# Attention gated per pair of heads and stored beside the chunk gate's part, so that each out-projection tile loads one contiguous block

## The chip, the cores and the metric

One NeuronCore of a Trainium2 chip runs the whole program. The metric is the device time of one launch in microseconds (us). Three runs of the kernel before gave 1382.57, 1385.22 and 1387.93 us; the median is 1385.22 us. Everything else about it is read from one profiled execution, whose own device time was 1381.67 us and whose trace spans 1379.9 us from the first to the last instruction.

## What is computed

One inference step of a decoder layer with two parallel groups: forgetting attention (8 heads of 64) and a chunk gate (4 channel groups of 128). Both are gated by a silu, joined to 1024 features and projected out. Cut to what matters here:

```python
def merge(x, attn, za, mix, u, zc, w_out):
    a = attn.reshape(B, S, D_ATT) * silu(za)               # 512 attention features
    m = (u * mix).reshape(B, S, D_CHK) * silu(zc)          # 512 chunk-gate features
    return x + concatenate([a, m], axis=-1) @ w_out        # 1024 x 1024
```

The prompt has 2048 positions; eight sample positions of a decode step (paged cache of 512 rows each) run through the same layer beside it. Everything is float32. The products keep float32 accuracy by splitting each operand into a rounded high part and the rest, and adding three matmuls (high by high, high by low, low by high).

## The kernel before

**Stages.** The input projection comes first (to about 580 us of the trace). It writes the attention queries, keys and values, and the chunk gate's result, to DRAM scratch. The loop over `UNITS` follows (about 600 to 1180 us): a unit is one head `h` and one chunk `c` of 512 queries, `values` (L933). The order of units is head after head, at the end (6,2), (7,0), (6,3), (7,1), (7,2), (7,3). Between a unit's matmuls the generator `fill` slips in filler work that writes the PSUM bank `fl`: what is left of the gate projections, then the out weights, then the first out-projection tiles. The last phase (1191.78 us to the end) has the remaining out-projection tiles, 14 of 16, in the banks `sc` and `av`, two of each, and the sample's own tile.

**Who sets the order.** TensorE's (PE's) instructions are in the order in which the Python code emits them. The other engines are ordered by a list scheduler, and each then works strictly in that order: an instruction that waits holds up all behind it. `later(ns, fn)` (L144) delays a piece of work until PE's counted clock has moved on by `ns`, and `pump` (L150) runs what has come due. `pump(all_=True)` runs everything that is waiting at once. After the last unit, L1249 does that, and tile 8 of the out-projection does it again (L1112).

**The attention part.** A unit leaves its unnormalised result in scratch `aT` (L981, features by positions). Its row sums are added up in `acc` by GpSimd (POOL, L965), turned by `add_up` (L983: four transposes of `acc` into a `tp` bank, a VectorE (DVE) reduction and a reciprocal `sm`, L988 and L989). 2000 ns later `done` (L991) turns the reciprocals, ScalarE (ACT) copies them out (`rt`, L995), and SyncE (SP), whose queue issues nearly all transfers, stores 2 KB into scratch `rT` (L996). The three `tp` banks are shared with the running maxima of the scores (matmuls `tp<-k,q`, DVE reductions `mn`, L892).

**The out-projection.** A tile is 128 positions. `out_inputs` (L1045) issues six loads on SP's queue: `m4` from `mT` (chunk gate), `z4` from `zT` (the silu gate), `a4` from `aT`, twice `r4` from `rT` (each head's reciprocals broadcast to its 64 features) and `xy` (the residual `x`). The first five fetch a 128-column slice of a features-by-positions array, which is 512 contiguous bytes per row. `OLAG` (11000 ns) of PE's clock later, `parts` runs: POOL multiplies `z4` by `r4` (L1061), DVE multiplies `a4` by 0.5 and by that (L1065), ACT casts `m4` and `a4` to the high parts and DVE subtracts for the low parts (two casts and two subtractions of 128x512; helper `split`, L230 and L235), all into the tile `am`. `out_products` (L1071) then runs 24 matmuls for each half of 512 output features, and DVE adds the bank to `xy` (L1081), which frees the bank. `OAHEAD` = 3 tiles are asked for ahead. `load_out_weights` (L1023) loads and splits the out weights `wo`, `WOLAG` (7000 ns) after their loads.

**The chunk gate's part.** `zc_steps` (L489) ends with a store of 128 features by 512 positions to `mT`.

Of the kernel before, what the change touches and what calls it, by code (L numbers as in the profile page):

```python
# [19 lines left out]
P = 128  # L20
# [4 lines left out]
NH = 8  # L25
# [11 lines left out]
FILL = 0.50  # L37
FILL7 = 0.95
FLAG = 7000.0
WOLAG = 7000.0  # L40
WOSTEP = 1500.0
OLAG = 11000.0
SLAG = 3000.0
LAG = 6400.0
AVB = 8
# [12 lines left out]
OAHEAD = 3  # L58
KORDER = (4, 5, 6, 7, 0, 1, 2, 3)
WOENG = ('act',)  # L60
OFIRST = 1
PAIRS = (14,)
KSTART = 8
PACE = 800.0
# [11 lines left out]
def hymba_step(ctx, tc, x_prompt, x_sample, cache_k, cache_v, cache_logf, page_table, g_norm, w_in,  # L76
# [129 lines left out]
    qk_lo = dr.tile([2 * 512, SEQ], F32, name="qk_lo")  # L206
    v_st = dr.tile([NH, P, NT, HD], F32, name="v_st")
    mixT = dr.tile([512, SEQ], F32, name="mixT")
    mT = dr.tile([512, SEQ], F32, name="mT")
    zT = dr.tile([512, SEQ], F32, name="zT")  # L210
    aT = dr.tile([512, SEQ], F32, name="aT")
    kx = dr.tile([NH, 4, SEQ], F32, name="kx")
# [267 lines left out]
    def cols_of(t, f, cp):  # L480
        return t[f * P:(f + 1) * P, cp * 512:(cp + 1) * 512]

    def u_steps(unit, f0, f, cp, tag, mx):
        nc.sync.dma_start(mx, cols_of(mixT, f, cp))
        po = bank(tag)
        yield from feat_steps(po, unit, f0, cp)
        nc.vector.scalar_tensor_tensor(mx, mx, 0.5, po, op0=ALU.mult, op1=ALU.mult)

    def zc_steps(unit, f0, f, cp, tag, mx):  # L489
        po = bank(tag)  # L490
        yield from feat_steps(po, unit, f0, cp)
        sz = twice_silu(po)
        nc.gpsimd.tensor_tensor(mx, mx, sz, op=ALU.mult)
        nc.sync.dma_start(cols_of(mT, f, cp), mx)

    def za_steps(unit, f0, f, cp, tag):
        po = bank(tag)
# [131 lines left out]
    def decode_scores():  # L629
# [12 lines left out]
                yield DEC[0]  # L642
        nc.sync.dma_start(kept, keep)

    def decode_attention():
        keep = s8(t="keep")
        nc.sync.dma_start(keep[:, :512], kept)
        lfp, sc = gates_and_scores(keep)
        prT = keep[:, 512:896].rearrange("p (n m) -> p n m", n=NPG)
        nc.vector.memset(prT[:, :, BH:], 0.0)  # L650
        own = small(8)[:BH]
        nc.sync.dma_start(own[:, 0:1], tiny[0].rearrange("b (h o) -> (b h) o", o=1))
        nc.sync.dma_start(own[:, 1:2], tiny[1].rearrange("b (h o) -> (b h) o", o=1))
        yield 8000

        one, lfT, cc = (s2(t=t)[:BH] for t in ("one", "lfT", "cc"))
        nc.vector.memset(one, 1.0)
# [24 lines left out]
        pt = bank("tp")  # L682
        for g in range(NPG):
            transpose(pt[:, g * BH:(g + 1) * BH], lg[:, g * P:(g + 1) * P], ident[:BH, :BH])
        nc.scalar.copy(prT[:, :, :BH], pt[:, :NPG * BH].rearrange("p (n m) -> p n m", n=NPG))
        for b in range(B):
            hs = slice(b * NH, (b + 1) * NH)
            vb = s8(t="vb").rearrange("p (g f) -> p g f", g=NPG)
            page_loads(b, range(NPG), [(cv, lambda g: vb[:, g])])

            def summed(b=b, vb=vb):

                po = bank("tp")
# [3 lines left out]
                nc.scalar.copy(t, po)  # L697
                for g in range(NPG):
# [234 lines left out]
    def values(at):  # L933
# [3 lines left out]
        for kt in range(4 * c + 4):  # L937
# [31 lines left out]
            def step(kt=kt, p=p, n0=n0, acc=acc, c=c, st=st, at=at):  # L969

                if kt == 0:
                    st["av"] = bank("av")
                av, fin = st["av"], kt == 4 * c + 3
                e = kt % 2
                mm(av[e * HD:(e + 1) * HD, n0:], hd["vst"][:, kt], p[:, n0:], kt < 2, kt >= 4 * c + 2,
                   (512 - n0) * 0.844)
                if fin:
                    t = s2(t="at")
                    nc.scalar.copy(t[:HD], av[HD:])
                    nc.vector.tensor_tensor(t[:HD], t[:HD], av[:HD], op=ALU.add)  # L980
                    nc.sync.dma_start(aT[h * HD:(h + 1) * HD, c * 512:(c + 1) * 512], t[:HD])  # L981

                    def add_up():  # L983
                        pt = bank("tp")
                        for j in range(4):
                            transpose(pt[:, j * P:(j + 1) * P], acc[:, j * P:(j + 1) * P], ident)
                        rs = small(4)
                        nc.vector.tensor_reduce(rs, pt.rearrange("p (j k) -> p j k", j=4), axis=AX.X, op=ALU.add)  # L988
                        nc.vector.reciprocal(rs, rs)  # L989

                        def done():  # L991
                            pt = bank("tp")
                            transpose(pt[:4, :P], rs, ident)
                            t = s2(t="rt")[:4, :P]
                            nc.scalar.copy(t, pt[:4, :P])  # L995
                            nc.sync.dma_start(rT[h, c * 512:(c + 1) * 512].rearrange("(n p) -> n p", p=P), t)  # L996
                            if h == NH - 1:
                                finished[0] += 1
                                for i in range(OFIRST if finished[0] == 1 else 0):
                                    prepare(i)  # L1000
                        later(2000, done)
                    due[at % 2] = add_up
                    later(ACLAG, lambda: flush(at % 2, add_up))
# [35 lines left out]
        for n, k in enumerate(KORDER):  # L1039
            later(n * WOSTEP, lambda n=n, k=k: load(n, k))  # L1040

    def rows_of(t, t0):
        return t[:, t0:t0 + P].rearrange("(k p) t -> p k t", p=P)

    def out_inputs(i):  # L1045

        t0 = i * P
        az, xy = s4(t="az"), s4(t="xy")
        a4, z4 = (az[:, b * 512:(b + 1) * 512].rearrange("p (k t) -> p k t", k=4) for b in range(2))
        m4, r4 = (s2(t=t).rearrange("p (k t) -> p k t", k=4) for t in ("m4", "r4"))  # L1050
        nc.sync.dma_start(m4, rows_of(mT, t0))
        nc.sync.dma_start(z4, rows_of(zT, t0))
        nc.sync.dma_start(a4, rows_of(aT, t0))
        rv = rT[:, t0:t0 + P].rearrange("(k o) t -> o k t", o=2)
        for o in range(2):
            nc.sync.dma_start(r4[o * HD:(o + 1) * HD], rv[o].partition_broadcast(HD))
        nc.sync.dma_start(xy, x[t0:t0 + P])
        got = {}

        def parts():  # L1060
            nc.gpsimd.tensor_tensor(z4, z4, r4, op=ALU.mult)  # L1061
            am = s8(F32R, "am")
            hi, lo = (am[:, r * D:(r + 1) * D].rearrange("p (k t) -> p k t", k=KT) for r in range(2))
            split(hi[:, 4:], lo[:, 4:], m4, "act")
            nc.vector.scalar_tensor_tensor(a4, a4, 0.5, z4, op0=ALU.mult, op1=ALU.mult)  # L1065
            split(hi[:, :4], lo[:, :4], a4, "act")
            got.update(hi=hi, lo=lo, xy=xy)
        later(OLAG, parts)
        return got
# [27 lines left out]
    def out_tiles():  # L1097

        gs = None
        for i in range(NT):  # L1100
# [8 lines left out]
            if i == 8:  # L1109
                for _ in Pe.steps:  # L1110
                    pass
                pump(all_=True)  # L1112
                gs = decode_out()
            if gs is not None and i < 12:
                next(gs, None)
# [130 lines left out]
                fill(m * dose)  # L1246
                pump()
    run_av(0)
    pump(all_=True)  # L1249
    hold[0] = 0.0  # L1250
    last_phase[0] = True
    for _ in fgen:
# [31 lines left out]
```

## Time and profile before

| | us |
|---|---|
| median of three runs | 1385.22 |
| the profiled execution: device time | 1381.67 |
| the profiled execution: span of the trace | 1379.9 |
| PE busy in the span (95%) | 1311.9 |
| DVE busy (51%) | 704.4 |
| POOL busy (41%) | 572.0 |
| ACT busy (31%) | 434.3 |
| share of time of the DMA engines on SP's queue | 44.2% |

The page gives the busy time of each engine and the mean clock that PE was granted (0.981 of full speed over the span). PE is busy nearly all the time, so what matters is where it is not, and where its clock is low. A row of the timeline reads: start, length, engine, line, operation, tile written and tiles read, shape, count, and in brackets how long the engine had stood still before it and what ended that. A row of the windows reads: the stretch, its length, then for each engine its busy time and number of instructions, PE's granted clock, the share of DMA time and GB/s.

### The profile page before, as it was taken

The page shows a single profiled execution, that of the slowest core. Times are in us where ns is not written, and L with a number is a line of the kernel's source. Part 1 is how long each engine was busy: PE and PEld are TensorE (multiplying, and loading weights), DVE is VectorE, ACT ScalarE, POOL GpSimd, SP SyncE. Part 2 cuts the span into 40 slices and gives each one's busy share as a digit, 9 for nine tenths or more (in the row PEclk, how much of TensorE's full clock was granted, in tenths as well). Part 3 has the DMA queues.
Part 4 walks back from the last instruction along what each step waited for, and adds up shares of the span by engine and source line. Part 5 has one row for each costly group of instructions (what it writes and reads, how often), then busy time and mean ns, then how long its engine had stood idle before and what let it go on. Part 6 is the DMA issues. An engine that isn't in the chain of part 4 may idle for free. (4 is left out here: it accounts for less than half of the span.)

```text
span 1379.9 us, 19555 instructions
## 1 busy us (share of the span) xinstructions
PE 1311.9 (95%) x6544; PEld 1007.3 (73%) x6544; DVE 704.4 (51%) x1344; ACT 434.3 (31%) x797; POOL 572.0 (41%) x679
## 2 busy tenths in 40 slices
PE   6999999999999999999999999999999888986998
PEld 5999999998887777766656656666665545665877
DVE  4446554535687444265675555555676643333221
ACT  5542322323222111133444444444553544110000
POOL 3113433323133555345755676567554454310000
PEclk9999999999999999999999999999999988998999
DMA  6644354645115566644325363544642543775401
GB/s 215 184 124 109 83 142 123 170 122 143 48 40 152 163 183 187 156 122 108 104 64 138 96 156 89 162 124 116 154 117 81 165 108 95 175 179 132 142 35 58
DMA packets 180791, 174.71 MB, mean 127 GB/s; under 512 B 39147, under 2 KB 141995, under 8 KB 179123
## 3 DMA queue, kind: packets, MB, share of 16 engines
q1 hardware_dynamic: 176802, 164.69, 44.2%
q10 hardware_dynamic: 3488, 8.39, 1.6%
q8 instruction: 52, 0.85, 0.3%
q14 instruction: 49, 0.39, 0.1%
q0 software_dynamic: 400, 0.38, 0.1%
HBM read 117.34 MB, written 56.08 MB: 126 GB/s over the span
## 5 line engine op out<-in xcount | busy, mean ns | idle before, releaser
L892 DVE TENSOR_REDUCE mn<-tp 128x1 f32<-128x384 f32 (+6 forms) x320 | 188.2, 604 | 126.8 <-PE tp L161 124.0
L952 ACT ACTIVATE p<-sc,zero 128x512 f32<-128x512 f32 (+1 forms) x320 | 196.5, 623 | 178.2 <-PE sc L161 171.7
L965 POOL TENSOR_TENSOR acc<-acc,p 128x512 f32<-128x512 f32 (+3 forms) x184 | 192.4, 1046 | 126.9 <-ACT p L952 116.6
L161 PE MATMUL acc<-wh,hh 128*128 128x384 f32 (+2 forms) x640 | 228.9, 358 | 0.0
L161 PE MATMUL acc<-wl,hh 128*128 128x384 f32 (+2 forms) x640 | 223.0, 348 | 1.2 <-DVE wl L243 1.2
L161 PE MATMUL acc<-wh,hl 128*128 128x384 f32 (+2 forms) x640 | 222.8, 348 | 0.6 <-DVE hl L235 0.6
L161 PE MATMUL sc<-q,k 128*128 128x512 f32 (+7 forms) x640 | 210.1, 405 | 3.3 <-ACT p L952 3.0
L161 PE MATMUL av<-p,vst 128*64 128x512 f32 (+3 forms) x640 | 139.4, 556 | 0.2 <-ACT p L952 0.2
L161 PEld LDWEIGHTS sc<-q,k 128*128 128x128 f32 (+1 forms) x640 | 117.3, 198 | 29.4 <-ACT p L952 12.6
L161 PE MATMUL tp<-k,q 66*128 66x384 f32 (+6 forms) x320 | 120.7, 392 | 6.3 <-ACT mt L914 4.9
L161 PEld LDWEIGHTS acc<-wh,hh 128*128 128x128 f32 x640 | 120.7, 189 | 7.4 <-ACT wh L240 0.2
L161 PEld LDWEIGHTS acc<-wl,hh 128*128 128x128 f32 x640 | 120.9, 189 | 6.7 <-DVE wl L243 2.1
L161 PEld LDWEIGHTS acc<-wh,hl 128*128 128x128 f32 x640 | 120.5, 188 | 6.3 <-DVE hl L235 1.1
L223 POOL TENSOR_SCALAR sm<-sm 128x6 f32<-128x6 f32 (+3 forms) x84 | 20.5, 244 | 238.2 <-DVE sm L376 170.7
L161 PEld LDWEIGHTS av<-p,vst 128*64 128x64 f32 x640 | 48.8, 140 | 70.6 <-issue 61.7
L161 PE MATMUL av<-wo,am 128*128 128x512 f32 x336 | 81.6, 400 | 11.6 <-DVE xy L1081 11.6
L224 POOL TENSOR_TENSOR sm<-sm,mhalf 128x6 f32<-128x6 f32 (+3 forms) x84 | 89.3, 1063 | 6.7
L161 PE MATMUL sc<-wo,am 128*128 128x512 f32 x336 | 80.4, 396 | 6.0 <-ACT am L230 4.8
L161 PEld LDWEIGHTS av<-wo,am 128*128 128x128 f32 x336 | 64.7, 194 | 27.0 <-DVE xy L1081 13.3
L161 PEld LDWEIGHTS tp<-k,q 66*128 66x128 f32 x320 | 61.7, 193 | 28.6 <-ACT mt L914 6.3
L161 PE MATMUL acc<-hh,wh 128*128 128x512 f32 x192 | 75.8, 395 | 4.2 <-DVE s L365 4.2
L161 PEld LDWEIGHTS sc<-wo,am 128*128 128x128 f32 x336 | 64.0, 191 | 20.4 <-ACT am L230 5.2
(220 smaller groups left out, 2102.5 us busy)
## 6 DMA issues: line engine op xcount, KB each, us to landing
raw<-in_w_in_dram SPq DMA_DIRECT2D x40, 256.0 KB
kb<-in_cache_k_dram SPq DMA_DIRECT2D x32, 256.0 KB
k<-qk_hi SPq DMA_DIRECT2D x16, 512.0 KB
q<-qk_hi SPq DMA_DIRECT2D x64, 128.0 KB
vb<-in_cache_v_dram SPq DMA_DIRECT2D x32, 256.0 KB
xy<-in_x_prompt_dram SPq DMA_DIRECT2D x16, 512.0 KB
out_dram<-xy ACTq DMA_DIRECT2D x15, 512.0 KB
xp<-in_x_prompt_dram SPq DMA_DIRECT2D x12, 512.0 KB
```

The source lines that it names most:

```text
L161: nc.tensor.matmul(out, lhsT, rhs, start=start, stop=stop)
L223: nc.gpsimd.tensor_scalar(r, ss, inv_n, EPS, op0=ALU.mult, op1=ALU.add)
L224: nc.gpsimd.tensor_tensor(r, r, mhalf[:rows, :n], op=ALU.pow)
L892: nc.vector.tensor_reduce(part[:, i % 4, n:n + 1], sp, axis=AX.X, op=ALU.min)
L952: nc.scalar.activation(p[:, n0:], sp[:, n0:], AF.Exp, bias=zero1, scale=-1.0)
L965: nc.gpsimd.tensor_tensor(acc[:, n0:], acc[:, n0:], p[:, n0:], op=ALU.add)
```

## The change

There are four parts.

1. **Gate per pair of heads.** When an odd head's `done` has stored its reciprocals, the new function `gate(k, c)` loads the pair's 128 features by 512 positions of `zT` and `aT` (rows of 2 KB) and the two heads' reciprocals. `GTLAG` (8000 ns) of PE's clock later it runs one POOL product, one DVE product and one store. There are 16 such gates, 13 of them among units and 3 at the end of the units and the start of the last phase.
2. **Storage by tiles.** The scratch `mT` becomes `gm[tile, feature in group, group, position]`. The chunk gate stores its groups 4 to 7 there, the gates store groups 0 to 3, both in pieces of 512 B. A tile of the out-projection is then one contiguous block of 512 KB.
3. **Out-projection inputs.** A tile issues two loads, `g` and `xy`, and one split of 128x1024. Its POOL product and its DVE product are gone. `OLAG` is 9000 instead of 11000, `WOLAG` 9000 instead of 7000, and two tiles instead of one are asked for as soon as the first chunk is finished (`OFIRST`).
4. **No flush.** After the last unit the waiting work is no longer run all at once, and at tile 8 only as much of it is run as the sample's attention needs.

```diff
-WOLAG = 7000.0
+WOLAG = 9000.0
-OLAG = 11000.0
+OLAG = 9000.0
+GTLAG = 8000.0
-OFIRST = 1
+OFIRST = 2
...
-    mT = dr.tile([512, SEQ], F32, name="mT")
+    gm = dr.tile([NT, P, KT, P], F32, name="gm")
...
+    def gm_of(k, c):
+        return gm[4 * c:4 * c + 4, :, k].rearrange("j p t -> p j t")
+    def by_tiles(t):
+        return t.rearrange("p (j t) -> p j t", j=4)
...
-        nc.sync.dma_start(cols_of(mT, f, cp), mx)
+        nc.sync.dma_start(gm_of(4 + f, cp), by_tiles(mx))
...
-                            if h == NH - 1:
-                                finished[0] += 1
-                                for i in range(OFIRST if finished[0] == 1 else 0):
-                                    prepare(i)
+                            if h % 2:
+                                gate(h // 2, c)
...
+    def gate(k, c):
+        a, z, r = s2(t="ga"), s2(t="gz"), s2(t="gr")
+        cs = slice(c * 512, (c + 1) * 512)
+        nc.sync.dma_start(z, cols_of(zT, k, c))
+        nc.sync.dma_start(a, cols_of(aT, k, c))
+        for o in range(2):
+            nc.sync.dma_start(r[o * HD:(o + 1) * HD], rT[2 * k + o, cs].partition_broadcast(HD))
+        def products():
+            nc.gpsimd.tensor_tensor(z, z, r, op=ALU.mult)
+            nc.vector.scalar_tensor_tensor(a, a, 0.5, z, op0=ALU.mult, op1=ALU.mult)
+            nc.sync.dma_start(gm_of(k, c), by_tiles(a))
+            if k == NH // 2 - 1:
+                finished[0] += 1
+                for i in range(OFIRST if finished[0] == 1 else 0):
+                    prepare(i)
+        later(GTLAG, products)
...
     def out_inputs(i):
-        nc.sync.dma_start(m4, rows_of(mT, t0))
-        nc.sync.dma_start(z4, rows_of(zT, t0))
-        nc.sync.dma_start(a4, rows_of(aT, t0))
-        rv = rT[:, t0:t0 + P].rearrange("(k o) t -> o k t", o=2)
-        for o in range(2):
-            nc.sync.dma_start(r4[o * HD:(o + 1) * HD], rv[o].partition_broadcast(HD))
-        nc.sync.dma_start(xy, x[t0:t0 + P])
+        g, xy = s4(t="g"), s4(t="xy")
+        nc.sync.dma_start(g, gm[i].rearrange("p k t -> p (k t)"))
+        nc.sync.dma_start(xy, x[i * P:(i + 1) * P])
...
         def parts():
-            nc.gpsimd.tensor_tensor(z4, z4, r4, op=ALU.mult)
             am = s8(F32R, "am")
-            split(hi[:, 4:], lo[:, 4:], m4, "act")
-            nc.vector.scalar_tensor_tensor(a4, a4, 0.5, z4, op0=ALU.mult, op1=ALU.mult)
-            split(hi[:, :4], lo[:, :4], a4, "act")
+            split(hi, lo, g, "act")
...
             if i == 8:
-                pump(all_=True)
+                while decoded[0] < B:
+                    Pe.waiting.pop(0)[2]()
...
     run_av(0)
-    pump(all_=True)
```

Three places in the order of instructions. The first is DVE in the last phase. Before, the rows for two consecutive bank releases and what stands between them were (L1081 adds a bank to `xy`, L1065 is the product on `az`, L235 subtracts for a low part; a row is its number on the engine, line, operation, tiles, shape):

```order
1296 L1065 SCALAR_TENSOR_TENSOR az_12670<-az_12670 128x512
1297 L1081 TENSOR_TENSOR xy_12101<-xy_12101,av_12346 128x512
1298 L235 TENSOR_TENSOR am_12752<-m_2331_12672,am_12752 128x512
1299 L235 TENSOR_TENSOR am_12752<-az_12670,am_12752 128x512
1300 L1081 TENSOR_TENSOR xy_12164<-xy_12164,sc_12383 128x512
1301 L1065 SCALAR_TENSOR_TENSOR az_12760<-az_12760 128x512
```

After the change the same stretch reads (its line numbers are those of the changed kernel, there up to 15 higher):

```order
1283 L1096 TENSOR_TENSOR xy_12110<-xy_12110,av_12360 128x512
1284 L236 TENSOR_TENSOR am_12696<-g_12643,am_12696 128x1024
1285 L1096 TENSOR_TENSOR xy_12196<-xy_12196,sc_12394 128x512
1286 L1096 TENSOR_TENSOR xy_12196<-xy_12196,av_12420 128x512
1287 L236 TENSOR_TENSOR am_12766<-g_12707,am_12766 128x1024
```

The product that waited for POOL no longer stands between the releases of two banks; one subtraction of double width is left.

The second place is DVE among the units, at the gate of heads 2 and 3 for the last chunk. Before, between the sum `at` of the attention result (L980) and the next maxima there was nothing:

```order
1062 L892 TENSOR_REDUCE mn_9996<-tp_10293 128x1
1063 L892 TENSOR_REDUCE mn_9996<-tp_10309 128x1
1064 L980 TENSOR_TENSOR at_10341<-at_10341,av_10332 64x512
1065 L892 TENSOR_REDUCE mn_9996<-tp_10352 128x1
1066 L903 TENSOR_REDUCE sm_10365<-mn_9996 128x4
```

After the change the gate's product (L1062, on `ga` and POOL's `gz`) stands there:

```order
1071 L903 TENSOR_REDUCE mn_10076<-tp_10389 128x1
1072 L991 TENSOR_TENSOR at_10428<-at_10428,av_10419 64x512
1073 L1062 SCALAR_TENSOR_TENSOR ga_10397<-ga_10397,gz_10398 128x512
1074 L903 TENSOR_REDUCE mn_10076<-tp_10439 128x1
1075 L914 TENSOR_REDUCE sm_10452<-mn_10076 128x4
```

The maxima that free PE's `tp` banks now stand behind a product that waits for the chain from `rt` over DRAM to POOL.

The third place is PE at the end of the units. Before, the last unit's four transposes of `acc` and its transpose of `sm` stood next to each other between two halves of an early out-projection tile (`fl`):

```order
5190 L161 MATMUL fl_12003<-wo_11174,am_11905 128x512 x3
5191 L165 MATMUL tp_12059<-ident,acc_6158 128x128 x4
5192 L165 MATMUL tp_12067<-ident,sm_12064 4x128
5193 L161 MATMUL fl_12073<-wo_11472,am_11905 128x512 x6
```

After the change they read:

```order
5193 L162 MATMUL fl_12157<-wo_11683,am_11739 128x512 x6
5194 L166 MATMUL tp_12179<-ident,acc_6158 128x128 x4
5195 L162 MATMUL fl_12157<-wo_11722,am_11739 128x512 x6
5196 L162 MATMUL sc_12199<-wo_11221,am_11982 128x512 x6
5197 L166 MATMUL tp_12206<-ident,sm_12184 4x128
```

Between the unit's last product with `vst` and the first of these transposes stand 24 matmuls instead of 3, and between the transposes of `acc` and that of `sm` 12 instead of none.

More of the change, by code (lines that the diff above doesn't have):

```diff
@@ L643, in decode_scores @@
         nc.sync.dma_start(kept, keep)
+    decoded = [0]
     def decode_attention():
@@ L697, in summed @@
                 nc.scalar.copy(t, po)
+                decoded[0] += 1
                 for g in range(NPG):
@@ L1040, in load_out_weights @@
             later(n * WOSTEP, lambda n=n, k=k: load(n, k))
-    def rows_of(t, t0):
-        return t[:, t0:t0 + P].rearrange("(k p) t -> p k t", p=P)
-    def out_inputs(i):
[L1047 to L1050, printed above, removed]
-        nc.sync.dma_start(m4, rows_of(mT, t0))
-        nc.sync.dma_start(z4, rows_of(zT, t0))
-        nc.sync.dma_start(a4, rows_of(aT, t0))
-        rv = rT[:, t0:t0 + P].rearrange("(k o) t -> o k t", o=2)
-        for o in range(2):
-            nc.sync.dma_start(r4[o * HD:(o + 1) * HD], rv[o].partition_broadcast(HD))
-        nc.sync.dma_start(xy, x[t0:t0 + P])
+    def gate(k, c):
[14 more added lines that the diff above has]
+        later(GTLAG, products)
@@ L1058, in out_inputs @@
+    def out_inputs(i):
+        g, xy = s4(t="g"), s4(t="xy")
+        nc.sync.dma_start(g, gm[i].rearrange("p k t -> p (k t)"))
+        nc.sync.dma_start(xy, x[i * P:(i + 1) * P])
         got = {}
         def parts():
-            nc.gpsimd.tensor_tensor(z4, z4, r4, op=ALU.mult)
             am = s8(F32R, "am")
-            hi, lo = (am[:, r * D:(r + 1) * D].rearrange("p (k t) -> p k t", k=KT) for r in range(2))
-            split(hi[:, 4:], lo[:, 4:], m4, "act")
-            nc.vector.scalar_tensor_tensor(a4, a4, 0.5, z4, op0=ALU.mult, op1=ALU.mult)
@@ L1066, in parts @@
-            split(hi[:, :4], lo[:, :4], a4, "act")
+            hi, lo = (am[:, r * D:(r + 1) * D] for r in range(2))
+            split(hi, lo, g, "act")
+            hi, lo = (t.rearrange("p (k t) -> p k t", k=KT) for t in (hi, lo))
             got.update(hi=hi, lo=lo, xy=xy)
```

## The prediction

> **What bounds the kernel now.** First the page's busy times, then a table of stretches, to see where PE stands still or is slow.
>
> ```profile
> PE 1311.9 (95%) x6544; PEld 1007.3 (73%) x6544; DVE 704.4 (51%) x1344; ACT 434.3 (31%) x797; POOL 572.0 (41%) x679
> ...
> 600.00:1000.00 400.00, 392.91 (x1974) 250.33 (x1974) 233.65 (x430) 176.47 (x321) 253.18 (x288) 1.00 0.47 122
> 1040.00:1050.00 10.00, 10.00 (x41) 5.53 (x40) 4.31 (x10) 2.41 (x7) 2.75 (x3) 0.70 0.47 142
> 1100.00:1110.00 10.00, 10.00 (x31) 5.54 (x31) 8.10 (x11) 4.93 (x9) 9.69 (x7) 0.50 0.56 177
> 1140.00:1150.00 10.00, 7.68 (x27) 4.99 (x27) 6.80 (x7) 5.12 (x11) 7.46 (x7) 0.58 0.36 86
> 1180.00:1192.00 12.00, 9.72 (x30) 7.32 (x31) 2.04 (x4) 0.87 (x2) 1.84 (x3) 0.72 0.90 218
> 1192.00:1376.00 184.00, 166.32 (x712) 132.52 (x710) 48.23 (x70) 13.89 (x24) 14.12 (x11) 0.96 0.42 115
> ```
>
> PE bounds the kernel. From 600 to 1000 us it is busy for 392.91 of 400 at full clock, so the change has little to win there and something to lose. After 1000 there are stretches with a granted clock of 0.50 to 0.72, and 17.7 idle us in the last phase (184.00 − 166.32). Next the timeline of PE, the stalls before the last phase (in brackets) and five rows of the last phase:
>
> ```profile
> 1039.42 0.37 PE L165 MATMUL tp<-ident,sm 128*4 128x128 f32 x1 [2.00 <-DVE sm L989]
> ...
> 1097.82 0.71 PE L161 MATMUL tp<-k,q 66*128 66x416 f32 x1 [4.58 <-ACT mt L914]
> ...
> 1142.32 0.38 PE L165 MATMUL tp<-ident,sm 128*4 128x128 f32 x1 [6.79 <-DVE sm L989]
> ...
> 1180.72 0.44 PE L165 MATMUL tp<-ident,acc 128*128 128x128 f32 x2 [1.28 <-POOL acc L967]
> 1181.52 0.33 PE L165 MATMUL tp<-ident,acc 128*128 128x128 f32 x1 [0.36 <-POOL acc L965]
> 1182.05 0.33 PE L165 MATMUL tp<-ident,acc 128*128 128x128 f32 x1 [0.20 <-POOL acc L965]
> 1183.38 0.37 PE L165 MATMUL tp<-ident,sm 128*4 128x128 f32 x1 [1.00 <-DVE sm L989]
> 1183.41 8.53 PE L161 MATMUL fl<-wo,am 128*128 128x512 f32 x24
> ...
> 1191.78 5.61 PE L161 MATMUL sc<-wo,am 128*128 128x512 f32 x24
> ...
> 1272.58 8.32 PE L161 MATMUL av<-wo,am 128*128 128x512 f32 x24 [9.01 <-DVE xy L1081]
> ...
> 1314.19 7.58 PE L161 MATMUL sc<-wo,amTs 128*40 128x512 f32 x32
> 1321.61 5.62 PE L161 MATMUL sc<-wo,am 128*128 128x512 f32 x24
> ...
> 1370.60 5.60 PE L161 MATMUL av<-wo,am 128*128 128x512 f32 x24
> ```
>
> At its best the last phase runs one half tile in 5.44 us: nine of them lie between the starts at 1321.61 and 1370.60. Then DVE, POOL and ACT, to see who holds PE up:
>
> ```profile
> 1271.23 0.69 DVE L1065 SCALAR_TENSOR_TENSOR az<-az 128x512 f32<-128x512 f32 x1 [13.46 <-POOL az L1061]
> 1271.84 0.68 DVE L1081 TENSOR_TENSOR xy<-xy,av 128x512 f32<-128x512 f32 x1
> ...
> 1269.94 1.26 POOL L1061 TENSOR_TENSOR az<-az,r 128x512 f32<-128x512 f32 x1 [20.52 <-DMA az<-zT]
> ...
> 1136.79 0.69 DVE L1065 SCALAR_TENSOR_TENSOR az<-az 128x512 f32<-128x512 f32 x1 [5.83 <-POOL az L1061]
> ...
> 1095.40 0.62 ACT L230 CAST wo<-raw 128x512 fp32r<-128x512 f32 x1 [5.99 <-DMA raw<-in_w_out_dram]
> ...
> DVE az L1065 <- POOL az L1061: 71.3, 13, 13.5
> ...
> POOL az L1061 <- DMA r<-rT: 60.7, 8, 17.8
> ```
>
> The chain is one: a late slice load holds POOL, POOL holds DVE's product, and behind it in DVE's order stands the addition that frees PE's bank (1271.23, 1271.84, then PE at 1272.58). DVE spent 71.3 us in 13 such waits.
>
> **The change part by part.**
>
> Last phase. The product that waits leaves DVE's order there, and with it the loads of 512-byte rows. The phase needs 28 half tiles of 5.44 us, 152.3, plus the sample's 7.4 (1314.19 to 1321.61) and 0.6 for its transposes: 160.3 us. It takes from 1191.78 to 1376.2 (1370.60 + 5.60), 184.4. So 24 us can go. What could be late next is the block `g`: 512 KB, with 512 KB of `xy` and a store of 512 KB per tile, 1.57 MB in 10.88 us or 145 GB/s. The stretch before 1192 moved 218 GB/s, so there is room, but single late loads stay possible. I take **−22**, with bounds −12 (half of it stays) and −24.
>
> End of the units. Without the flush PE no longer goes straight from the last products to `acc` and `sm`; 24 and 12 matmuls (at 0.227 us each, 5.44/24, that is 5.4 and 2.7 us) stand where it waited 1.28 + 0.36 + 0.20 + 1.00 = 2.84 us. The slow 24 matmuls after it lasted 8.53 − 5.44 = 3.1 us too long. Together 5.9. POOL now has a gate's product of 1.26 us between the last unit's sums, which may eat some. **−4**, bounds 0 and −6.
>
> The stall of 6.79 us at 1142. DVE's `sm` stood behind the product that waited 5.83 us at 1136.79, one of those that leave. In the stretch behind it PE was busy for 7.68 us at 0.58, so 0.42 × 7.68 = 3.2 us were lost as well. Gates stand near that place too (their own price is below). **−8**, bounds −3 and −10.
>
> The stalls of 4.58 us at 1097 and 2.00 at 1039. At 1097 ACT's copy `mt` stood behind a cast of out weights that waited 5.99 us for its load; 10 us at clock 0.50 followed, 5 us lost, 9.6 together. At 1039 DVE was occupied by the weights' subtractions; with 0.30 × 10 = 3 us of lost clock that is 5. `WOLAG` gives those loads 2 us more, and an out tile puts two loads ahead of them on SP instead of six. Whether the list scheduler's new places are covered no row shows. **−6** of 14.6, bounds 0 and −14.6.
>
> A rule of the skill speaks to these lost clocks. The Trainium skill, TensorE: Matmul & The Clock Gate, section What's actually happening, has the clock fall only after an idle window of about 3.4 us. By it the wait of 2.00 us would cost 2 and not 5, and each short stall of a gate (below) nothing beyond itself. The trace speaks against it: clock 0.70 in the 10 us behind a single wait of 2.00 us.
>
> Gates among the units. This is the new cost. Each gate adds four loads and a store on SP, 1.29 us on POOL and 0.69 on DVE. POOL is busy 253 of 400 us and DVE 234 there, so work alone is covered. The wait is not. The gate of the second place in the order runs against these rows:
>
> ```profile
> 975.01 0.27 PE L165 MATMUL tp<-ident,sm 128*4 128x128 f32 x1
> ...
> 975.52 0.24 ACT L995 COPY rt<-tp 4x128 f32<-4x128 f32 x1
> ...
> 975.78 0.24 SPq L996 DMA_DIRECT2D rT<-rt  x1
> ...
> 980.44 0.68 DVE L980 TENSOR_TENSOR at<-at,av 64x512 f32<-64x512 f32 x1 [4.53 <-ACT at L979]
> 981.43 0.69 DVE L892 TENSOR_REDUCE mn<-tp 128x1 f32<-128x512 f32 x1 [0.32 <-PE tp L161]
> ...
> 980.93 0.39 PE L161 MATMUL tp<-k,q 66*128 66x512 f32 x1
> ...
> 982.81 0.42 PE L161 MATMUL tp<-k,q 66*128 66x384 f32 x1
> ...
> 844.46 0.61 SPq L916 DMA_DIRECT2D mrow<-mt  x2
> ...
> 846.03 0.22 SPq L862 DMA_DIRECT2D q<-mrow  x1
> ...
> 1224.69 1.12 SPq L554 DMA_DIRECT2D ps<-p_s  x1
> ...
> 1228.59 0.69 DVE L1065 SCALAR_TENSOR_TENSOR az<-az 128x512 f32<-128x512 f32 x1 [5.96 <-DMA ps<-p_s]
> ...
> 1247.46 1.30 SPq L1056 DMA_DIRECT2D r<-rT  x2
> ...
> 1261.11 0.55 SPq L1052 DMA_DIRECT2D az<-zT  x1
> ```
>
> DVE reaches the gate's product at 981.1 (980.44 + 0.68). The store of the reciprocals is issued by 976.0. In the 5.1 us between, 2 KB must land, two loads be issued (1.30) and land, and POOL multiply (1.26). The store: the equally small `mrow` was issued by 845.1 and read at 846.0, so 1.0 us. The loads: 16 KB of `ps` landed in 2.8 us (1225.8 to 1228.6), 256 KB of `zT` in 512-byte pieces behind other loads in 8.3 (1261.7 to 1269.9). A gate's reciprocals are 2 KB rows, nearer to the first; I take 3 us. Then POOL is done at 976.0 + 1.0 + 1.3 + 3.0 + 1.3 = 982.6, and DVE waits 1.5 us. Behind it stand the maxima that free the three `tp` banks. The reduction of the bank that PE filled at 980.93 would end at 982.1, and PE wants that bank again, after two others, at 982.81: 0.7 us of cover. PE stands still for 0.8 us. POOL's sums wait too, but after the last sum of a unit POOL had idle time. With 13 gates among units that is **+10**; the three at their end are in the bounds above. The near end is 0, where the loads land 1.5 us sooner; the far end, 8.3 us at each gate, is the first rival.
>
> A second rule weighs on the gates. The Trainium skill, SBUF — State Buffer, section The DMA setup-cost knee, puts a roughly fixed 2 us on every transfer however small, mostly until its landing is confirmed. By it the two landings are 4 us, as in my 1.0 + 3.0, and the sum stays as it is; the trace agrees for the load (2.8 us) and not for the store (1.0 us).
>
> Sum: −22 −4 −8 −6 +10 = **−30**. Against the profiled execution, 1381.7 − 30 = 1351.7. That execution was 3.5 us below the median of the runs shown, so on the median it is 1385.2 − 30 = 1355; I say **1353**. With all terms at their good ends (−24 −6 −10 −14.6 + 0 = −54.6) it would be 1327 to 1331. With the gains at their bad ends (−12 + 0 −3 + 0) and the gates as forecast it would be −5, 1377 to 1380.
>
> **The rivals.**
>
> *Gates stall PE (slower).* The reciprocals land so late that PE stands still for 2 us or more at a gate, and the clock falls: 2 + 3 = 5 us by the row at 1039. With 10 of 13 gates hit, +50 against −40 makes 1381.7 + 10 = **1392**. It decides from eight gates on (8 × 5 = 40). That needs a DVE wait of 0.7 + 2 = 2.7 us, loads that land in 4.2 us instead of 3. For it speak the 8.3 us of `zT`, and that the three tiles of a gate take turns in the pool of 11 that ACT and DVE use for everything else; against it that those were small pieces behind two other loads, and that places later than this one have more room. Chance 0.10.
>
> *The last phase stays bound by its loads.* The blocks `g` come late because `xy`, the out stores and the last gates' loads share the DMA engines. Half of the 24 us stays, the weights' stalls stay, the gates cost as forecast: 1381.7 − 12 − 4 − 8 + 10 = **1368**. For it: DMA share 0.90 just before the phase. Against: 218 GB/s in the same row, and 145 needed. Chance 0.20.
>
> *The wait only moves.* The change does what it says, −40, but the gates' waits for POOL and DMA give back 25 to 40 us among the units: **1367** to the old time. Chance 0.14, of which 0.08 lies within 0.5% of before.
>
> *Forecast*, 1335 to 1362: chance 0.56.
>
> **How the numbers follow.** 0.5% is 6.9 us, about what a measurement of this kernel can tell from no change. Faster by more: 0.56 + 0.20 + 0.06 = 0.82; within: 0.08; slower: 0.10. The range goes from 1335, short of the good ends, to 1381; it leaves out the slower rival, some of the cases near the old time and a little below, 0.2 in all.
>
> **What would show it.** Right: PE's rows of the last phase 5.6 us long with starts 5.44 apart and no bracket above 1 us, the phase some 161 us long; no wait of DVE on a product between two L1096 rows; the waits at 1039, 1097, 1142 and 1181 gone or under 1.5 us. For the gates: DVE L1062 waiting for POOL 1 to 2 us each, some 20 us in all, and PE's idle time between 600 and 1000 up from 7.1 us by less than 10. Wrong: PE waits on `tp` banks above 2 us with a granted clock below 1.00 in that stretch, or ACT waiting for DMA `g` in the last phase.

## The result, and the profile after

The changed kernel takes 1394.3 us (median of 11 runs, 1387.04 to 1400.39), the kernel before 1383.26 us in the same sessions (11 runs, 1374.66 to 1387.93). The ratio is 1.0084 with a 95% interval of 1.0058 to 1.0110: slower by 0.8%, where 1353 was forecast. The profiled execution of the changed kernel took 1399.12 us, its span is 1397.4 us, 17.5 more than before. The medians lie 11.0 us apart, so some 6 us of these 17.5 are scatter from one execution to the next; what follows accounts for the profiled pair.

First the windows of the changed kernel, for the units and for its last phase (columns as before).

```profile
600.00:1000.00 400.00, 377.97 (x1819) 241.97 (x1817) 226.09 (x400) 161.72 (x294) 245.81 (x278) 0.96 0.49 131
...
1233.00:1394.00 161.00, 160.62 (x713) 129.87 (x711) 37.31 (x47) 8.92 (x11) 1.29 (x1) 1.00 0.26 90
```

The last phase has become what the forecast wanted: PE is busy for 160.62 of 161 us at full clock. From 600 to 1000 us, where PE stood still for 7.1 us before, it now stands still for 22.0, and its granted clock is 0.96 instead of 1.00, so in 400 us it gets 1819 matmuls done instead of 1974. The timeline of PE around the start and the end of the last phase:

```profile
1232.73 1.52 PE L162 MATMUL sc<-wo,am 128*128 128x512 f32 x6
...
1388.02 5.60 PE L162 MATMUL av<-wo,am 128*128 128x512 f32 x24
```

The phase starts 41.0 us later than before (1232.73 against 1191.78) and lasts 160.9 us (to 1393.62) instead of 184.4. 41.0 − 23.5 = 17.5 is the whole difference of the spans. So the question is where 41 us went before the last phase. Both kernels turn each unit's reciprocals on PE (`tp<-ident,sm`) in the same order, which makes a clock for the comparison. Eight of these times and the two ends of the last phase:

| before, us | changed, us | lag, us |
|---|---|---|
| 676.9 | 678.6 | 1.7 |
| 719.6 | 728.8 | 9.1 |
| 844.4 | 859.3 | 14.9 |
| 897.2 | 915.0 | 17.8 |
| 916.8 | 947.2 | 30.4 |
| 975.0 | 1006.5 | 31.5 |
| 988.9 | 1025.0 | 36.1 |
| 1084.9 | 1132.6 | 47.7 |
| 1191.8 (last phase) | 1232.7 | 41.0 |
| 1376.2 (its end) | 1393.6 | 17.5 |

The lag grows by 46 us until 1085 us of before, in steps behind gates. One of the steps, 5.0 us up to the reciprocals turned at 1033.1 before, has another wait in it: PE waited 2.17 us for ACT's `p` (1073.35), which stood behind a cast of out weights that had waited 3.25 us for its load; whether a gate made that load late is not shown. Behind 1085 the waits at 1097 and 1142 and at the end of the units give some of the lag back.

Two windows show of what the lag is made. They reach from 600 us to the reciprocals of the row 1084.9, in the kernel before and in the changed kernel:

```profile
600.00:1084.88 484.88, 474.90 (x2368) 302.71 (x2368) 290.15 (x525) 216.34 (x394) 294.67 (x327) 0.99 0.45 120
```

```profile
600.00:1132.57 532.57, 500.23 (x2377) 317.84 (x2376) 308.36 (x541) 217.57 (x397) 312.44 (x339) 0.94 0.48 130
```

Of the 47.7 us more, 22.4 are PE standing still (32.3 us instead of 10.0). The other 25.3 are PE working longer on nearly the same matmuls, at a granted clock of 0.94 instead of 0.99. PE's list of waits says on whom it waits:

```profile
PE tp L162 <- DVE mn L903: 16.5, 9, 4.8
PE sc L162 <- ACT p L963: 12.4, 9, 3.9
...
PE tp L166 <- POOL acc L976: 6.0, 4, 2.3
```

In the kernel before, the wait for `DVE mn` in the first row was 0.2 us.

The gate of the forecast's example shows the chain. It is the gate of heads 4 and 5 for the first chunk (above it is called that of heads 2 and 3 for the last), and its reciprocals were turned at 975.0 before and at 1006.5 now. The rows are from the timelines of PE, SP, POOL and DVE:

```profile
1006.51 0.27 PE L166 MATMUL tp<-ident,sm 128*4 128x128 f32 x1
...
1007.27 0.24 SPq L1007 DMA_DIRECT2D rT<-rt  x1
1009.02 0.34 SPq L1056 DMA_DIRECT2D ga<-aT  x1
1009.41 1.36 SPq L1058 DMA_DIRECT2D gr<-rT  x2
...
1013.68 1.27 POOL L1061 TENSOR_TENSOR gz<-gz,gr 128x512 f32<-128x512 f32 x1 [2.68 <-DMA gr<-rT]
...
1014.98 1.73 DVE L1062 SCALAR_TENSOR_TENSOR ga<-ga,gz 128x512 f32<-128x512 f32 x1 [2.38 <-DMA q<-qk_hi]
...
1017.37 0.44 PE L162 MATMUL tp<-k,q 66*128 66x384 f32 x1 [2.88 <-DVE mn L903]
```

DVE stood at the gate's product for 2.38 us. The row puts that wait down to a load, but the product starts 0.03 us after POOL's ends (1013.68 + 1.27), which is what it waited for. Then the product took 1.73 us, the maxima behind it came late, and PE waited 2.88 us for a `tp` bank. From this gate to the next unit's reciprocals the lag grew by 4.6 us, so 1.8 us came as slow clock behind the wait; the granted clock was 0.83 from 1015 to 1025 us. The worst gate is the one at 915:

```profile
913.18 5.99 SPq L710 DMA_DIRECT2D o_s<-ob  x4
919.76 0.34 SPq L1055 DMA_DIRECT2D gz<-zT  x1
920.20 0.26 SPq L1007 DMA_DIRECT2D rT<-rt  x1
...
921.78 1.69 SPq L1058 DMA_DIRECT2D gr<-rT  x2
...
927.88 1.26 POOL L1061 TENSOR_TENSOR gz<-gz,gr 128x512 f32<-128x512 f32 x1 [10.81 <-DMA gr<-rT]
...
929.17 1.73 DVE L1062 SCALAR_TENSOR_TENSOR ga<-ga,gz 128x512 f32<-128x512 f32 x1 [7.45 <-POOL gz L1061]
...
932.16 0.58 PE L162 MATMUL tp<-k,q 66*128 66x256 f32 x1 [4.82 <-DVE mn L903]
```

Here the reciprocals were ready at 915.8 (ACT's copy), but four stores of the sample's attention held SP's queue for 5.99 us, then the loads landed 4.4 us after their issue. DVE waited 7.45 us and PE 4.82. PE also waited 2.26 and 1.13 us for POOL's sums (941.39 and 942.85), and its granted clock from 913 to 950 us was 0.82. The lag grew by 12.6 us from 915.0 to 947.2. Not all of it is the products': `no_products` (below) loses 3.7 us in the same place without them.

### The profile page after: what moved, and what is told of

It reads as the page before. It is cut to its first block, busy times and chain, and to the rows that moved or that the text cites. A ratio compares the mean times of both kernels' runs of the same rounds, so it can differ in the third digit from the quotient of the medians.

```text
span 1397.4 us, 19555 instructions
## 1 busy us (share of the span) xinstructions
PE 1330.4 (95%) x6544; PEld 1020.1 (73%) x6544; DVE 714.2 (51%) x1328; ACT 431.0 (31%) x781; POOL 576.7 (41%) x679
## 4 chain that ended last, share of the span: by engine, by line
PE 80%; DMA 7%; DVE 5%; POOL 2%; issue 2%; ACT 2%; SPq 1%; ACTq 0%; POOLq 0%; DVEq 0%
PE acc L162 34%; PE sc L162 14%; PE av L162 13%; PE fl L162 9%; PE tp L162 5%; PE tp L166 4%; PE pm L162 1%; DMA gr<-rT 1%; ACT p L963 1%; DVE mn L903 1%; DMA raw<-in_w_in_dram 1%; DVE ga L1062 1%; DMA xp<-in_x_prompt_dram 1%; DVE wl L244 1%; DMA rT<-rt 1%
## 5 line engine op out<-in xcount | busy, mean ns | idle before, releaser
L976 POOL TENSOR_TENSOR acc<-acc,p 128x512 f32<-128x512 f32 (+3 forms) x184 | 197.1, 1071 | 125.6 <-ACT p L963 111.1
L162 PE MATMUL sc<-q,k 128*128 128x512 f32 (+7 forms) x640 | 216.3, 416 | 12.6 <-ACT p L963 12.4
L162 PEld LDWEIGHTS sc<-q,k 128*128 128x128 f32 (+1 forms) x640 | 121.5, 204 | 38.3 <-ACT p L963 20.2
L162 PE MATMUL av<-p,vst 128*64 128x512 f32 (+3 forms) x640 | 143.3, 569 | 0.0
L162 PE MATMUL tp<-k,q 66*128 66x384 f32 (+6 forms) x320 | 125.5, 406 | 18.2 <-DVE mn L903 16.5
L162 PEld LDWEIGHTS tp<-k,q 66*128 66x128 f32 x320 | 64.7, 202 | 42.1 <-DVE mn L903 20.9
L162 PE MATMUL av<-wo,am 128*128 128x512 f32 x336 | 78.4, 389 | 0.0
L162 PE MATMUL acc<-hl,wh 128*128 128x512 f32 x192 | 75.6, 394 | 0.0
L162 PE MATMUL fl<-hh,fh 128*128 128x512 f32 x176 | 75.5, 429 | 0.0
```

The source lines that it names most:

```text
L162: nc.tensor.matmul(out, lhsT, rhs, start=start, stop=stop)
L976: nc.gpsimd.tensor_tensor(acc[:, n0:], acc[:, n0:], p[:, n0:], op=ALU.add)
```

## The experiments

All times are medians, ratios are to the kernel before, run beside them on the same chip. The runs are from several chips, and the kernel before took 1379.0 to 1382.4 us beside them, so times of different runs compare to within a few us.

**early_r** takes the reciprocals' way over DRAM out of the wait.

```diff
-            nc.sync.dma_start(r[o * HD:(o + 1) * HD], rT[2 * k + o, cs].partition_broadcast(HD))
+            nc.sync.dma_start(r[o * HD:(o + 1) * HD], zT[k * P + o * HD, cs].partition_broadcast(HD))
```

> The gate's two loads of reciprocals take rows of the silu gate instead (written long before, same shapes and bytes), so the attention part is not normalised; PE's order is unchanged and nearly all of the other engines' too. Theory (DVE and POOL wait in their order for the reciprocals' way over DRAM, store and load, and PE waits behind them for tp banks): these waits go, the 48 us lost up to 1127 us of the trace fall below 10, the time is 1394 - 40 = about 1354. Rival (the loss is the added traffic on the DMA engines, the three more tiles per gate, or DVE and POOL working at the same time): same instructions, same bytes, so 1390 to 1398.

Measured: 1394.7 us, ratio 1.0106 (1.0082 to 1.0130). The theory missed. POOL's waits for this load in the changed kernel, then here:

```profile
POOL gz L1061 <- DMA gr<-rT: 57.9, 10, 24.2
```

```profile
  DMA gr<-zT: 44.1, 11
```

The load still lands late, since SP issues it at the same place in its queue, behind the loads of `gz` and `ga`. The store's landing is a small part: in the changed kernel SP waited for it before 8 loads, 10.9 us in all, here not at all, and the time is the same.

**gt16** waits longer before the products.

```diff
-GTLAG = 8000.0
+GTLAG = 16000.0
```

> GTLAG 16000 instead of 8000, nothing else. Theory: POOL waited 0.6 to 10.8 us for the reciprocals at 10 gates; 8 us more on PE's clock cover all but one or two, the time is 1350 to 1362. Rival (traffic, tiles): 1390 or more, and since a gate holds its three of the eleven tiles for 8 us longer, perhaps 1400.

Measured: 1389.2 us, ratio 1.0058 (1.0031 to 1.0084), which overlaps the changed kernel's. Not the forecast, for a plain reason: the delay did not arrive. The order of DVE's 1328 instructions differs from that of the changed kernel in a dozen rows, and all 16 products stand behind the same number of maxima as before. `later` delays when the work is written down; where it stands on DVE and POOL the list scheduler decides by its own estimate of when the operands are there.

**dve_first** changes which product waits for the reciprocals.

```diff
-            nc.gpsimd.tensor_tensor(z, z, r, op=ALU.mult)
             nc.vector.scalar_tensor_tensor(a, a, 0.5, z, op0=ALU.mult, op1=ALU.mult)
+            nc.gpsimd.tensor_tensor(a, a, r, op=ALU.mult)
```

> DVE multiplies 0.5 * a * z first, which waits for no reciprocal, and POOL multiplies by r afterwards; same results up to rounding. Theory in its narrow form (DVE's place in line is what stops PE, since PE waited for DVE's maxima on the tp banks): the 16.5 us of PE waiting for mn fall to 1 or 2, with the slow clock behind them about 30 us are won, 1360 to 1370. If POOL's place in line is as bad (its sums late, PE waiting for acc and for p), only about half of it, 1375 to 1385. Rival (traffic, tiles): 1390 to 1398.

Measured: 1360.3 us, ratio 0.9843 (0.9815 to 0.9870), as the narrow form had it. PE's wait for maxima fell, though to 5.2 us and not to 1 or 2:

```profile
PE tp L162 <- DVE mn L903: 5.2, 10, 1.3
```

DVE still waits here, 38.4 us at 12 gates for `ga`. But the product now ends 5.1 to 11.5 us after the reciprocals are turned (median 7.8 over 13 gates) instead of 7.8 to 15.9 (median 10.4). So what counts seems to be when the product is done against when PE wants a bank, not the sum of DVE's waits. The product is also short here (0.69 us in the median), which this run does not separate.

**before_noflush** is the kernel before with the fourth part alone: the two `pump(all_=True)` of the out-projection go, and tile 8 runs the waiting work until the sample's attention is complete.

> The kernel before with the fourth part of the change alone: no flush after the last unit, and at tile 8 only what the sample's attention needs. By the forecast's term the stop at the end of the units goes, 4 us, and the last phase keeps its 24 us of waiting: 1377 to 1381 against 1383. If the out tiles' inputs, no longer drawn together, come later, the last phase waits longer: 1385 to 1395.

Measured: 1376.6 us, ratio 0.9966 (0.9946 to 0.9986): a gain of 0.3%, some 4 us. The amount is that of the term, the way is not: PE now waits 7.41 us for `sm` at 1197.20 and 7.84 for `DVE xy` at 1248.78, instead of 9.01 at 1272 and the stop at 1181. With the old loads the waits change places.

**no_products** leaves out the two products of a gate (`tensor_tensor` and `scalar_tensor_tensor` in `gate`).

> The gates keep all loads and stores but leave out both products (the attention part is stored ungated), so nothing on DVE or POOL waits for a gate. Theory (products that stand in line for late loads): the whole loss goes, with the last phase at its best 1340 to 1350. Rival (the added transfers slow everything else): still above 1375.

Measured: 1358.0 us, ratio 0.9841 (0.9798 to 0.9884). With all transfers of the gates in place, the loss is nearly gone: the lag at the row 1084.9 is 6.1 us instead of 47.7. So the added traffic is not the main cause. The expected 1340 to 1350 was too good.

**loads_early** issues `gz` and `ga` at the end of the odd head's unit.

```diff
                     nc.sync.dma_start(aT[h * HD:(h + 1) * HD, c * 512:(c + 1) * 512], t[:HD])
+                    if h % 2:
+                        gate_loads(h // 2, c)
```

> The changed kernel with the gate's loads of aT and zT issued at the end of the odd head's unit, right behind the store to aT, and only the reciprocals loaded behind their store; products and their places in line the same. Theory that four loads issued in a bunch land late (512 KB ahead of the reciprocals in the queue): POOL's wait for gr falls from 58 us to 25 or less, time 1365 to 1380. If the reciprocals' own way over DRAM is what is late, POOL's wait stays above 45 us and the time above 1388.

Measured: 1391.3 us, ratio 1.0074 (1.0049 to 1.0098): the time is that of the second expectation, the wait that of neither. POOL's wait for `gr` fell to 42.2 us only, and DVE's wait for POOL was 50.0 us instead of 43.7.

**dve_first_early** joins the two.

> Both: loads of aT and zT early, DVE's product first. Theory: DVE's waits for ga (38 us in dve_first) fall below 15 us and only POOL still waits; 1345 to 1355, the fastest of all. Rival (DVE's wait was covered in dve_first, POOL's is what is left): the same as dve_first, 1358 to 1363.

Measured: 1406.2 us, ratio 1.0185 (1.0149 to 1.0221), the opposite of the forecast. With the loads written earlier, the scheduler puts DVE's products 1 to 6 maxima further forward than in `dve_first`. At 12 of the 13 gates DVE now starts the product before the reciprocals are turned, and it stands ahead of the reductions and reciprocals of row sums (`sm`). PE waits for those:

```profile
PE tp L162 <- DVE sm L1001: 13.9, 8, 3.5
PE tp L166 <- DVE sm L1002: 12.1, 7, 4.8
```

**pool_both** takes DVE out of the gates.

```diff
-                            nc.scalar.copy(t, pt[:4, :P])
+                            nc.scalar.activation(t, pt[:4, :P], AF.Copy, scale=0.5)
...
-            nc.gpsimd.tensor_tensor(z, z, r, op=ALU.mult)
-            nc.vector.scalar_tensor_tensor(a, a, 0.5, z, op0=ALU.mult, op1=ALU.mult)
+            nc.gpsimd.tensor_tensor(a, a, z, op=ALU.mult)
+            nc.gpsimd.tensor_tensor(a, a, r, op=ALU.mult)
```

> Both products on POOL (the factor 0.5 goes into the copy of the reciprocals), DVE has nothing of the gates; loads as in the changed kernel. If DVE's place in line is the whole harm: as fast as dve_first or up to 5 us faster, 1355 to 1362, although POOL works 1.3 us more per gate. If POOL's waits and its added work hurt as well: 1365 to 1380.

Measured: 1353.8 us, ratio 0.9814 (0.9773 to 0.9855), faster than both kernels. POOL waits for the loads as DVE did, and works 1.3 us more per gate:

```profile
POOL ga L1061 <- DMA ga<-aT: 35.5, 8, 14.5
POOL ga L1061 <- DMA gr<-rT: 13.7, 5, 5.8
```

PE's waits show that this costs little, and none of it at the maxima above 1.1 us:

```profile
PE sc L162 <- ACT p L963: 9.4, 11, 2.7
PE tp L166 <- POOL acc L976: 6.2, 5, 2.8
...
PE tp L162 <- DVE mn L903: 1.3, 2, 1.1
```

**const_products** keeps both engines' work and nearly its places, but on a constant (`bsb`), so that nothing waits for a load.

```diff
+            b, w = bsb.rearrange("p g t -> p (g t)"), s2(t="gw")
-            nc.gpsimd.tensor_tensor(z, z, r, op=ALU.mult)
-            nc.vector.scalar_tensor_tensor(a, a, 0.5, z, op0=ALU.mult, op1=ALU.mult)
+            nc.gpsimd.tensor_tensor(w, b, b, op=ALU.mult)
+            nc.vector.scalar_tensor_tensor(w, b, 0.5, w, op0=ALU.mult, op1=ALU.mult)
```

> All loads and stores of the gates stay, and both products run on POOL and DVE in nearly the same places in line (0 to 8 of the 320 maxima later), but on a constant that is in SBUF from the start, so neither waits for a load; the attention part is stored ungated. Theory (the waiting in line is the harm): PE's wait for mn falls below 4 us and the time to 1355 to 1365, as without products (1358). Rival (the harm is the work itself: DVE's product took 1.73 us instead of 0.69 in 12 of 16 gates, beside POOL): DVE's products stay at 1.7 us and the time above 1380.

Measured: 1365.7 us, ratio 0.9903 (0.9876 to 0.9930). The median is just above the expected 1355 to 1365, far from the rival's 1380. PE's wait for maxima was 6.5 us, not below 4, and 4.7 of it stood at one place: DVE's product waited 4.59 us there for POOL's, which stood behind POOL's other work, and PE's lag grew by 6.8 us. DVE's products took 0.69 us in the median. Transfers and work are all there, and 29 us of the changed kernel's 1394.3 are gone. Against `no_products`, 7.6 us remain, most of them at this one place, so the work itself costs little.

**all_early** has all four loads at the end of the unit.

> As loads_early, and the reciprocals' loads too, which take rows of the silu gate instead (no wait for a store; attention part not normalised). The scheduler then puts the products 0 to 6 maxima further forward. Theory that what counts is when the product can start on the chip, measured from its place in line: the loads have 5 to 7 us more, the place moves forward by 0 to 6 of them, so a part of the loss stays: 1360 to 1385, and DVE's wait for POOL below 30 us. If the loads' landing alone counted, not the place: 1355 to 1360.

Measured: 1410.4 us, ratio 1.0200 (1.0169 to 1.0231). The prediction of 1360 to 1385 missed. The products moved forward by up to 7 maxima, five of the 13 even ahead of the turning of the reciprocals, and waited there as long as before (DVE for POOL 48.3 us):

```profile
PE tp L166 <- DVE sm L1002: 23.4, 4, 8.0
```

**pool_both_early** is `pool_both` with the loads of `loads_early`.

> pool_both with the loads of aT and zT issued at the end of the odd head's unit. POOL waited 35 us for ga in pool_both; if POOL's waits cost anything, the time falls by 3 to 8 us below 1354; if they are covered by its idle time, 1352 to 1356. If POOL's first product moves forward before the unit's last sums, as DVE's did, and stands there waiting, PE waits for acc: above 1360.

Measured: 1383.0 us, ratio 1.0007 (0.9987 to 1.0027). The third outcome: POOL's first product moves forward by up to 6 of POOL's sums, stands there waiting, and PE waits for those sums, 12.4 us instead of 6.2 (and 15.4 us instead of 9.4 for ACT's `p`):

```profile
PE tp L166 <- POOL acc L976: 12.4, 8, 3.4
```

So POOL's place in line is not harmless in itself; it is in `pool_both`, where the products stand later.

**pool_both_consts** sets `WOLAG` and `OLAG` of `pool_both` back.

> pool_both with WOLAG and OLAG back at 7000 and 11000. If the delays only shift when work is written down and the scheduler sets the places (with GTLAG 16000 the orders of DVE, ACT and POOL differed from those with 8000 in 5 to 12 rows): within 3 us of pool_both, 1351 to 1357. If the 2 us more for the out weights' loads carried the term of 6 us in the forecast: 1358 to 1362, with the waits of ACT's casts for raw and of PE for mt back.

Measured: 1357.9 us, ratio 0.9838 (0.9813 to 0.9862), within the interval of `pool_both`. The expected waits of ACT's casts and of PE for `mt` did not come back (ACT waited 4.3 us for `raw` in all, 3.6 in `pool_both`). What these two constants are worth stays below what this measurement can tell.

## Why the prediction was wrong

**The last phase** (−22): right. 184.4 us became 160.9, −23.5; the forecast's 160.3 was the floor it came to. DVE still waited 6.7 us there for the last gate's product, without a wait of PE.

**The end of the units, the stalls at 1142, 1097 and 1039** (−4, −8, −6): alone, the missing flush gave about 4 us. In the changed kernel only 6.7 us of these came back (lag 47.7 to 41.0), because new waits stand there. PE waited 3.93 us for ACT's `p` at 1209: ACT's queue stood at the store of a finished tile, whose addition on DVE came behind a gate's product that had waited 8.23 us. It waited 2.97 us at 1148, where ACT's cast of a block `g` had waited 2.07 us for its load. The stall at 1039 did not go: PE waited 2.00 us for `DVE sm` again, at 1089.23. In `pool_both`, without DVE in the gates, the last phase starts at 1187.77, 4.0 us earlier than before. The same unit's reciprocals that were turned at 1084.9 were turned there at 1095.0, so 14.1 us came back between the two. The three terms have 18 together, so their sum was about right. The reason given first for the −6, `WOLAG`, is not borne out: `pool_both_consts` sets it back, and the wait for `mt` stays away.

**The gates among the units** (+10): this is the step that failed, by a factor of four and a half; it was 46 us. The mechanism was the one named, DVE standing at a product that waits for POOL. Its price was wrong twice over. The forecast had 13 waits of PE of 0.8 us, and PE stood still for 22.4 us more than before; and it had nothing for the slow clock behind these waits, which was nearly all of the other 25.3 us. The example gate and the others show where this comes from:

1. The way of the reciprocals: I had 1.0 us from the store's issue to the loads' issue, there were 1.9 (1007.51 to 1009.41). The landing, which I had taken for the doubtful part, was 2.9 us against 3.0.
2. DVE's product took 1.73 us, not 0.69, since POOL started a sum at the same moment (below). Together DVE was 0.9 + 1.0 us later than forecast, and PE's wait was 2.88 and not 0.8.
3. I had priced the slow clock only in the rival, above 2 us of waiting. The forecast gate crossed that line by itself, and the line does not hold either: the clock fell behind shorter waits too (below).
4. One example carried all 13. From the turning of the reciprocals to the start of DVE's product it forecast 7.6 us; measured were 8.5 there, and 6.4 to 14.1 at the 13 gates (median 8.6). DVE stood still before these 13 products for 34.8 us, where some 20 were forecast. The long end comes from SP's queue (four stores ahead, 5.99 us), which had no term, and one such gate cost 12.6 us.

The first rival gave 1392 for just this mechanism; 1394 was measured. It had a chance of 0.10, on the ground that its landings were worst cases. The landings needed no worst case, since the longer product and the later issue did it. That its number came so close is in part luck: it counted ten gates with 2 us of waiting or more, and PE waited as long for the maxima at four (852, 932, 1017 and 1037), while one gate cost 12.6 us instead of 5 and the gains were smaller than its −40.

**What the experiments settle.** Without the products the loss goes (`no_products`), without DVE's share it goes (`pool_both`), with the work but without waiting for loads most of it goes (`const_products`). Transfers and work are thereby excluded as the main cause. One more queue is held up by the gates: SP issues a gate's store only when the product is done, and the loads behind it wait as well. In the changed kernel SP waited 50.0 us for `DVE ga` in this way. In `pool_both` it still waited 29.3 us for `POOL ga`, with the loss gone, so this is not the main cause either. Issuing loads earlier does not help: in `loads_early` the products kept their places and POOL still waited for the reciprocals, and in `dve_first_early` and `all_early` the scheduler moved the products forward. `GTLAG`, which reads like time that covers the chain, covers nothing (`gt16`). The forecast had not counted on it: it took the product's place from the order of DVE, and that was right.

**What stays open.** `pool_both` is still slower among the units than the kernel before: its lag is 10.1 us at 1084.9. `no_products` has 6.1 there, so most of it comes without any product; how much of the rest is POOL's lateness (8.4 us of waits for `acc`) was not separated. How the loss divides between waiting and the longer product was not separated either: a product that does not wait is usually also short. At the two gates among the units with the short product DVE waited 2.59 and 3.10 us, and the lag grew by 1.5 us and not at all. Three with the long product and waits of 2.38, 2.83 and 4.00 cost 4.6, 8.7 and 4.7 us. This points at the longer product, but one with a wait of 6.75 us and a long product cost only 1.5.

## What to carry to other kernels

Work that waits for a transfer should stand on the engine whose queue nobody waits for just then: with the gates on DVE and POOL this change cost 0.8%, with the gates on POOL alone it won 1.9%. When a list scheduler sets the order, a delay in the source or an earlier load need not make room; it may move the waiting instruction forward, and the order has to be looked at again with the measured landings beside it. And when a new wait of the bounding engine is priced, its clock behind the wait belongs in the price: here it was as large as the waits themselves, and the forecast had it at nothing.

## What the runs showed of the hardware

DVE's product of two tiles in SBUF takes 0.69 us alone and 1.73 us when POOL has just started an addition. The two cases, each with POOL's rows and DVE's, in the timelines of the changed kernel:

```profile
848.72 1.29 POOL L1061 TENSOR_TENSOR gz<-gz,gr 128x512 f32<-128x512 f32 x1 [2.79 <-DMA q<-qk_hi]
849.97 1.26 POOL L970 TENSOR_TENSOR acc<-p 128x512 f32<-128x512 f32 x1
...
850.04 1.73 DVE L1062 SCALAR_TENSOR_TENSOR ga<-ga,gz 128x512 f32<-128x512 f32 x1 [4.00 <-POOL gz L1061]
```

```profile
865.69 1.30 POOL L1061 TENSOR_TENSOR gz<-gz,gr 128x512 f32<-128x512 f32 x1 [2.41 <-DMA gr<-rT]
...
867.02 0.69 DVE L1062 SCALAR_TENSOR_TENSOR ga<-ga,gz 128x512 f32<-128x512 f32 x1 [2.59 <-POOL gz L1061]
```

In the first, POOL's overdue sum starts with DVE's product, since both waited for POOL's product to end, and DVE ends 0.54 us after it; in the second POOL has nothing to do. At 13 of 16 gates a POOL operation overlapped, and only the three without one took 0.69 us. So a product that starts just as POOL goes on to its next sum costs DVE one microsecond more. The Trainium skill, SBUF — State Buffer, section Who interferes with whom, says that a DVE instruction with two inputs in SBUF contends with a GpSimd instruction that reads SBUF. The trace agrees.

The length of a single wait did not tell whether the clock would fall. It fell behind a wait of 2.32 us (until 852.43): it was 0.71 in the ten us from 850. It also fell behind one of 1.61 us (until 696.49): it was 0.50 in the ten us from 697.2.

```profile
697.20:707.20 10.00, 9.32 (x26) 6.27 (x27) 7.72 (x19) 2.33 (x5) 3.17 (x3) 0.50 0.36 113
...
850.00:860.00 10.00, 7.68 (x30) 5.52 (x28) 8.37 (x16) 2.09 (x5) 2.50 (x3) 0.71 0.52 151
```

Behind a wait of 1.46 us (until 724.37) it was 0.57 from 724 to 728 us. In the kernel before it stayed at 1.00 from 716 to 726 us, behind a wait of the same 1.46 us (until 715.91).
